# RMSNorm and projection with Strassen-like products: crossbar transposes in three pieces, and a new order for the head

## The chip, the cores and the metric

The kernel runs on one core of one Trainium2 chip. The metric is device time in microseconds (us) of one execution. A run consists of several executions, and the median of three is given for the kernel before.

## The reference

`x` has the shape (8, 1024, 768), that is 8192 rows of 768; `w_qkv` is 768 x 2304; all in float32. Each row is divided by its root mean square, scaled by `gamma`, and multiplied by the weights:

```python
rms = np.sqrt(np.mean(x ** 2, axis=-1, keepdims=True) + eps)
x_norm = x / rms * gamma
return np.matmul(x_norm, w_qkv).astype(np.float32)
```

The output is 8192 x 2304 in float32, 75.5 MB; the input is 25.2 MB, the weights 7.1 MB.

## The kernel before, in words

**Tiles.** The rows are cut into 64 tiles of 128. `load_x` (line 371) brings a tile in through SP's DMA queue. `load_w` (376) brings the weights in 16 pieces, and `conv` (382 to 386) multiplies them by `gamma` and makes them bf16, on VectorE, ScalarE or GpSimd as its last argument says.

**Tiles 0 to 3** go the plain way: cast, transpose on TensorE, `mm` against the bf16 weights (line 450, 512 or 256 columns), `evac` with the row's scale, `store`.

**Tiles 4 to 63** go in 30 pairs (2 to 31). A pair's 256 rows and 768 contraction elements form a 2 x 2 matrix of blocks; the weights, in three column chunks `c` of 768, form another. Seven products of blocks instead of eight give the result (Winograd's form of Strassen's algorithm). For the weights, `bound`, `fold`, `bound_tr`, `bound_top`, `bound_all` and `scales` find one scale per chunk, `quad` (548 to 552) makes four f16 quadrants, and `tsum` (558) four differences of quadrants. For the rows, `pstat` and `prms` on ScalarE and `precip` on VectorE give the row scales; `pcast` (582, VectorE) writes the scaled tile as f16 into `xb`; `pxbar` (586) transposes it by DMA from `xb` to `xT`, a crossbar transpose of 128 x 768; `osum` (600) makes the four sums s1 to s4 of `xT` blocks, on GpSimd in the steady state. s1 needs the whole odd tile, s4 comes last. `product` (620) is three matmuls of 128 x 384 into PSUM; products 1, 2 and 4 read `xT` itself, 5, 6, 3 and 7 read s1, s2, s4 and s3. `hold` (627, 629), `join` (638) and `last` (642) take results out of PSUM, and `pstore` (648) writes 384 KB, or half of it, to the output.

**What sets the order.** Every operation is entered with a time, and operations are emitted sorted by it. The time is only a sort key: each engine then runs its instructions in that order as their inputs come. For the first pairs the keys stand in a list, `PLAN`, which also delays some stores of early tiles to the end of the head. From pair 12 (`STEADY`) on a rule gives them: pair p and chunk c begin at z = `HEAD_END` + 7 slots for each chunk since pair 12, where a slot (three matmuls) is 0.4875 us, so that a pair has 21 slots or 10.24 us; everything else stands at z plus so many slots. All DMAs of tiles, weights, transposes and outputs are issued by SP, in one queue. Buffers: 9 of `x_t`, 4 of `xb`, 10 of `xT`, 3 of the sums, 12 of `ot`.

Of the kernel before, what the change touches and what calls it, by code (L numbers as in the profile page):

```python
# [15 lines left out]
HEAD_END = 134.61  # L16
# [3 lines left out]
    (0.000, "load_x", 1), (1.100, "load_x", 2), (1.460, "load_w", 4), (1.820, "load_x", 0), (2.180, "load_x", 3),  # L20
    (4.790, "cast", 1, "DVE"), (4.791, "gamma_in"), (4.792, "load_w", 2), (4.793, "stat", 1), (6.130, "recip", 1),
    (6.131, "load_w", 3), (6.132, "cast", 2, "ACT"), (6.440, "conv", 4, 5, "POOL"), (6.441, "idle", 3),
    (6.442, "load_w", 1), (6.820, "stat", 2), (6.821, "load_w", 0), (9.081, "conv", 2, 3, "POOL"), (9.082, "stat", 3),
    (9.083, "load_w", 6), (9.084, "idle", 6, 512), (9.085, "tr", 1), (9.086, "cp", 1, "DVE"),
    (9.761, "conv", 3, 4, "POOL"), (9.762, "stat", 0), (11.722, "conv", 0, 0, "ACT"), (11.723, "cast", 0, "DVE"),
    (11.724, "load_w", 7), (11.725, "cast", 3, "DVE"), (11.726, "conv", 1, 2, "POOL"), (11.727, "idle", 5, 512),
    (11.728, "mm", 1, 0, "5"), (11.729, "tr", 2), (11.730, "tr", 0), (11.731, "cp", 2, "DVE"), (11.732, "tr", 3),
    (11.733, "mm", 2, 0, "5"), (11.734, "mm", 1, 0, "3"), (11.735, "cp", 0, "DVE"), (11.736, "mm", 2, 0, "3"),
    (11.737, "mm", 0, 0, "5"), (11.738, "mm", 0, 0, "3"), (11.739, "mm", 0, 0, "4"), (11.740, "mm", 1, 0, "4"),
    (11.741, "recip", 0), (11.742, "cp", 3, "DVE"), (11.743, "mm", 2, 0, "4"), (11.744, "mm", 1, 0, "2"),  # L30
    (13.042, "conv", 6, 2, "POOL"), (13.043, "conv", 0, 1, "DVE"), (13.044, "mm", 0, 0, "2"),
    (13.045, "mm", 0, 0, "01"), (13.046, "bound", 0, 1, "DVE"), (13.047, "mm", 1, 0, "01"),
    (13.365, "mm", 2, 0, "012"), (13.832, "recip", 2), (13.833, "conv", 6, 3, "ACT"), (13.972, "bound", 0, 0, "ACT"),
    (14.013, "mm", 0, 512, "23"), (14.444, "mm", 1, 512, "23"), (14.445, "load_w", 5), (15.572, "evac", 1, 0, "ACT"),
    (15.573, "evac", 2, 0, "DVE"), (15.574, "mm", 2, 512, "23"), (15.575, "conv", 7, 5, "DVE"),
    (15.576, "conv", 7, 4, "POOL"), (15.577, "evac", 0, 0, "DVE"), (15.578, "mm", 3, 512, "23"),
    (15.739, "mm", 0, 512, "54"), (16.171, "mm", 3, 512, "45"), (16.172, "load_w", 9), (16.173, "conv", 5, 0, "DVE"),
    (16.603, "mm", 1, 512, "45"), (16.604, "conv", 5, 1, "POOL"), (16.605, "bound", 0, 2, "ACT"),
    (17.035, "mm", 3, 512, "01"), (17.036, "bound", 1, 0, "DVE"), (17.466, "mm", 2, 512, "45"),
    (17.467, "conv", 9, 3, "POOL"), (17.898, "mm", 1, 512, "01"), (17.899, "load_w", 8), (18.330, "mm", 2, 512, "01"),  # L40
    (18.761, "mm", 0, 512, "01"), (18.762, "fold", 0), (18.763, "conv", 8, 0, "ACT"), (19.193, "bound_tr", 0),
    (19.194, "conv", 9, 2, "POOL"), (19.195, "evac", 1, 512, "DVE"), (19.513, "bound_top", 0),
    (19.514, "mm", 3, 1024, "23"), (19.745, "mm", 0, 1024, "23"), (20.177, "bound_all", 0),
    (20.178, "conv", 8, 1, "POOL"), (20.179, "evac", 2, 512, "ACT"), (20.180, "bound", 1, 1, "ACT"),
    (20.297, "mm", 0, 1024, "01"), (20.298, "load_w", 10), (20.728, "mm", 2, 1024, "23"),
    (20.729, "conv", 10, 4, "POOL"), (20.730, "recip", 3), (20.731, "evac", 3, 512, "DVE"), (20.732, "load_x", 5),
    (20.733, "scales", 0), (20.953, "evac", 0, 512, "DVE"), (20.954, "load_w", 13), (21.160, "mm", 1, 1024, "23"),
    (21.613, "quad", 0, "b12", "DVE"), (21.614, "conv", 10, 5, "POOL"), (22.353, "conv", 13, 5, "DVE"),
    (22.354, "mm", 2, 1024, "01"), (22.355, "bound", 1, 2, "ACT"), (22.356, "mm", 0, 1024, "45"),
    (22.455, "mm", 2, 1024, "45"), (22.456, "load_w", 12), (22.783, "evac", 0, 1024, "DVE"),  # L50
    (22.784, "quad", 0, "b22", "POOL"), (23.443, "fold", 1), (23.444, "mm", 1, 1024, "01"),
    (23.445, "mm", 3, 1024, "45"), (23.446, "load_x", 4), (23.750, "mm", 3, 1024, "01"), (24.182, "bound_tr", 1),
    (24.183, "quad", 0, "b11", "DVE"), (24.184, "pstat", 5), (24.502, "bound_top", 1),
    (24.503, "conv", 13, 4, "POOL"), (24.504, "evac", 3, 1024, "ACT"), (24.722, "tsum", 0, "t1", "DVE"),
    (24.723, "load_w", 11), (24.724, "mm", 0, 1536, "45"), (24.733, "mm", 1, 1024, "45"),
    (25.587, "conv", 11, 0, "DVE"), (25.588, "pstat", 4), (25.952, "conv", 11, 1, "ACT"), (25.953, "load_x", 6),
    (25.954, "conv", 12, 2, "POOL"), (25.955, "bound_all", 1), (26.017, "tsum", 0, "t3", "DVE"),
    (26.018, "mm", 2, 1536, "45"), (26.592, "prms", 2), (26.593, "mm", 1, 1536, "45"),
    (26.594, "conv", 12, 3, "POOL"), (26.842, "evac", 1, 1024, "ACT"), (26.843, "mm", 3, 1536, "45"),
    (26.844, "mm", 1, 1536, "23"), (27.012, "mm", 3, 1536, "23"), (27.444, "mm", 0, 1536, "01"),  # L60
    (27.875, "mm", 0, 1536, "23"), (27.876, "evac", 2, 1024, "ACT"), (27.877, "load_w", 15), (27.878, "load_x", 7),
    (28.042, "pstat", 6), (28.043, "precip", 2), (28.044, "pcast", 4), (28.045, "scales", 1), (29.012, "pstat", 7),
    (29.013, "mm", 2, 1536, "23"), (29.014, "load_w", 14), (29.015, "pcast", 5), (29.016, "pxbar", 4),
    (29.017, "mm", 1, 1536, "01"), (29.018, "tsum", 0, "t2", "POOL"), (29.019, "pxbar", 5),
    (29.982, "evac", 1, 1536, "ACT"), (29.983, "conv", 15, 4, "DVE"), (29.984, "quad", 0, "b21", "POOL"),
    (29.985, "conv", 15, 5, "POOL"), (29.986, "mm", 3, 1536, "01"), (29.987, "conv", 15, 3, "POOL"),
    (29.988, "mm", 2, 1536, "01"), (30.034, "mm", 3, 0, "012345"), (30.035, "bound", 2, 1, "DVE"),
    (30.582, "prms", 3), (30.583, "evac", 0, 1536, "DVE"), (31.242, "precip", 3), (31.482, "pcast", 6),
    (32.032, "pcast", 7), (32.033, "mm", 3, 2048, "345"), (32.034, "load_x", 10), (32.035, "load_x", 11),
    (32.036, "mm", 2, 2048, "345"), (32.037, "conv", 14, 1, "POOL"), (32.172, "pxbar", 6),  # L70
    (32.173, "mm", 1, 2048, "345"), (32.174, "conv", 14, 0, "POOL"), (32.175, "conv", 14, 2, "POOL"),
    (32.582, "evac", 3, 0, "DVE"), (33.242, "osum", 2, "s1", "DVE"), (33.243, "mm", 2, 2048, "012"),
    (33.244, "store", 1, 1, 1024, 1024), (33.562, "osum", 2, "s3", "DVE"), (33.563, "mm", 0, 2048, "345"),
    (33.564, "product", 2, 0, 1), (33.882, "osum", 2, "s2", "DVE"), (33.883, "bound", 2, 0, "ACT"),
    (33.884, "pxbar", 7), (33.885, "load_x", 12), (33.886, "mm", 0, 2048, "012"), (33.887, "mm", 3, 2048, "012"),
    (33.888, "evac", 3, 1536, "ACT"), (34.202, "evac", 2, 2048, "DVE"), (34.203, "mm", 1, 2048, "012"),
    (34.204, "load_x", 13), (34.436, "product", 2, 0, 2), (34.602, "evac", 0, 2048, "DVE"),
    (34.924, "product", 2, 0, 5), (34.925, "quad", 1, "b12", "POOL"), (34.926, "hold", 2, 0, "a", "p1", "ACT"),
    (35.124, "join", 2, 0, 0, 0, "b", "p1"), (35.125, "bound", 2, 2, "ACT"), (35.411, "product", 2, 0, 6),
    (35.412, "load_x", 9), (35.413, "quad", 1, "b11", "POOL"), (35.899, "product", 2, 1, 1),  # L80
    (35.900, "evac", 1, 2048, "ACT"), (35.901, "fold", 2), (35.902, "quad", 1, "b22", "POOL"),
    (36.144, "hold", 2, 0, "c", "p5", "ACT"), (36.145, "osum", 2, "s4", "DVE"), (36.386, "product", 3, 1, 1),
    (36.874, "bound_tr", 2), (36.875, "evac", 3, 2048, "ACT"), (36.876, "tsum", 1, "t1", "DVE"),
    (36.877, "quad", 1, "b21", "POOL"), (37.194, "bound_top", 2), (37.195, "product", 3, 0, 1),
    (37.481, "product", 2, 0, 3), (37.482, "hold", 2, 0, "a", "u2", "ACT"), (37.483, "tsum", 1, "t2", "DVE"),
    (38.114, "osum", 3, "s3", "DVE"), (38.115, "hold", 2, 1, "a", "p1", "ACT"), (38.116, "product", 2, 1, 5),
# [216 lines left out]
def kernel(  # L303
# [8 lines left out]
    nc = tc.nc  # L312
# [14 lines left out]
    P = 128  # L327
# [412 lines left out]
```

## Time and profile before

| | us |
|---|---|
| median of 3 runs | 375.63 (372.15 to 376.89) |
| the profiled execution | 373.2 |
| its span in the profile | 371.1 |

| engine | busy us | share of the span |
|---|---|---|
| TensorE matmul (PE) | 345.1 | 93% |
| VectorE (DVE) | 275.0 | 74% |
| ScalarE (ACT) | 247.0 | 67% |
| GpSimd (POOL) | 145.5 | 39% |

The profile is one execution. Its page has the busy share of each engine in 40 slices of the span, the DMA queues, the chain of work that ended last (followed back from the last instruction, at each step to what released it) and the costliest groups of instructions by source line. The trace behind the page can be asked for instructions in order of time, for busy time in chosen stretches, and for waits. SPq is SP's queue: its rows are the issuing of DMAs, not their transfer. The times from issue to landing are in the page's last part:

```profile
out_dram<-ot SPq DMA_DIRECT2D x178, 384.0 KB, 4.9
x_t<-in_x_dram SPq DMA_DIRECT2D x64, 384.0 KB, 5.3
...
xT<-xb SPq DMA_TRANSPOSE x60, 5.4
```

The queue that carries them all is in the third part (packets, bytes, and the time that their packets took, as a share of 16 engines' span):

```profile
q1 hardware_dynamic: 89248, 119.56, 99.2%
```

### The profile page before, as it was taken

What the parts mean: (1) busy time and instruction counts of PE and PEld (TensorE: products, weight loads), DVE (VectorE), ACT (ScalarE), POOL (GpSimd) and SP (SyncE); (2) the same over time, 40 slices, a digit from 0 to 9 for tenths busy, and PEclk for the clock granted to TensorE, in tenths of its full rate; (3) what the DMA queues carried; (4) which work ended last, traced back from release to release, by engine and by line L of the source; (5) the groups of instructions that cost most, each with busy time, mean ns of one, the idle gap of its engine ahead of it and who ended that gap; (6) DMA issues with size and microseconds to landing.
All of it is one profiled execution on the core that took longest, in us unless ns stands there. A gap on an engine that the chain in (4) does not pass through costs nothing.

```text
span 371.1 us, 6579 instructions
## 1 busy us (share of the span) xinstructions
PE 345.1 (93%) x2055; PEld 199.6 (54%) x2055; DVE 275.0 (74%) x482; ACT 247.0 (67%) x495; POOL 145.5 (39%) x151
## 2 busy tenths in 40 slices
PE   5899796989799989999699999999999999999994
PEld 2445353555456546565366665666666666666662
DVE  2789999867467657777287777788787878777762
ACT  4697675657647757577367766776776677677543
POOL 1479795433132134430344423242444444345300
PEclk9999999999989999999899999999999999999999
DMA  7995986999989999999999999999999999997765
GB/s 256 391 388 133 310 323 189 300 267 388 256 320 356 294 392 394 307 378 347 395 309 377 350 304 356 335 388 331 354 362 336 347 344 377 316 380 259 253 256 213
DMA packets 89294, 119.98 MB, mean 323 GB/s; under 512 B 52390, under 2 KB 54188, under 8 KB 89260
## 3 DMA queue, kind: packets, MB, share of 16 engines
q1 hardware_dynamic: 89248, 119.56, 99.2%
q8 instruction: 16, 0.26, 0.3%
q14 instruction: 18, 0.15, 0.1%
q10 hardware_dynamic: 12, 0.00, 0.0%
HBM read 32.25 MB, written 75.50 MB: 290 GB/s over the span
## 4 chain that ended last, share of the span: by engine, by line
PE 67%; DMA 22%; DVE 6%; issue 2%; POOL 1%; SPq 1%; ACT 0%; DVEq 0%; POOLq 0%
PE pm L620 67%; DMA xT<-xb 8%; DMA out_dram<-ot 7%; DMA wq<-in_w_qkv_dram 5%; DVE xb L582 2%; DVE ot L638 2%; DMA x_t<-in_x_dram 2%; POOL su L600 1%; DVE su L600 1%; DVE bnd L507 0%; DVE wq L558 0%; DVE ot L466 0%; DVE w_b L382 0%; SPq L371 0%; DVE os L466 0%
## 5 line engine op out<-in xcount | busy, mean ns | idle before, releaser
L620 PE MATMUL pm<-wq,su 128*128 128x384 f16 x1080 | 208.3, 329 | 7.3 <-POOL su L600 5.1
L638 DVE SCALAR_TENSOR_TENSOR ot<-pm,sc,pp 128x384 f32<-128x384 f32 x270 | 155.4, 613 | 55.1 <-PE pm L620 40.3
L620 PE MATMUL pm<-wq,xT 128*128 128x384 f16 x810 | 162.5, 327 | 8.3 <-DVE ot L638 6.9
L629 ACT ACTIVATE pp<-pm,sc 128x384 f32<-128x384 f32 x214 | 121.0, 581 | 68.5 <-PE pm L620 61.8
L620 PEld LDWEIGHTS <-su 128*128 128x128 f16 x1080 | 105.3, 99 | 82.2 <-POOL su L600 8.0
L600 POOL TENSOR_TENSOR su<-xT 128x384 f16<-128x384 f16 x54 | 51.3, 970 | 183.4 <-DMA xT<-xb 131.7
L620 PEld LDWEIGHTS <-xT 128*128 128x128 f16 x810 | 79.2, 98 | 61.9 <-issue 10.3
L642 ACT ACTIVATE ot<-pm,sc 128x384 f32<-128x384 f32 x90 | 52.3, 581 | 41.2 <-PE pm L620 39.2
L582 DVE TENSOR_SCALAR xb<-x_t,rstd 128x768 f16<-128x768 f32 x60 | 52.4, 875 | 1.0
L627 DVE TENSOR_SCALAR pp<-pm,sc 128x384 f32<-128x384 f32 x56 | 34.3, 614 | 24.8 <-PE pm L620 24.6
L568 ACT ACTIVATE sq<-x_t 128x768 bf16<-128x768 f32 x60 | 50.0, 834 | 0.3 <-DMA x_t<-in_x_dram 0.3
L600 POOL TENSOR_TENSOR su<-xT,su 128x384 f16<-128x384 f16 x28 | 28.4, 1014 | 3.3 <-DVE su L600 1.2
L450 PE MATMUL pm<-w_b,xT 128*128 128x512 bf16 (+1 forms) x120 | 25.0, 358 | 1.1 <-ACT w_b L384 0.6
L600 POOL TENSOR_TENSOR su<-su,xT 128x384 f16<-128x384 f16 x27 | 25.0, 927 | 0.0
L386 POOL TENSOR_SCALAR w_b<-wq,g_sb 128x512 bf16<-128x512 f32 (+1 forms) x20 | 13.6, 692 | 13.3 <-DMA wq<-in_w_qkv_dram 13.3
L450 PEld LDWEIGHTS <-xT 128*128 128x128 bf16 x120 | 11.3, 98 | 12.7 <-issue 2.0
L558 POOL TENSOR_TENSOR wq<-wq 128x1152 f16<-128x1152 f16 x6 | 15.0, 2500 | 4.3 <-DVE wq L558 4.2
L552 POOL TENSOR_SCALAR wq<-w_b,inv 128x1152 f16<-128x1152 bf16 x9 | 12.8, 1430 | 2.5 <-DVE inv L536 2.5
L568 ACT ACTIVATION_READ_ACCUMULATOR sq<-x_t 128x1 f32 x60 | 11.5, 191 | 0.0
L510 ACT ACTIVATE sq<-w_b 128x1536 bf16<-128x1536 bf16 x6 | 8.9, 1475 | 1.2 <-DVE w_b L382 1.1
L572 ACT ACTIVATE rms<-ssq,eps_sb 128x2 f32<-128x2 f32 x30 | 8.8, 295 | 0.9
L466 DVE TENSOR_SCALAR ot<-pm,rstd 128x512 f32<-128x512 f32 x8 | 5.9, 742 | 0.4 <-PE pm L450 0.3
(47 smaller groups left out, 68.5 us busy)
## 6 DMA issues: line engine op xcount, KB each, us to landing
out_dram<-ot SPq DMA_DIRECT2D x178, 384.0 KB, 4.9
x_t<-in_x_dram SPq DMA_DIRECT2D x64, 384.0 KB, 5.3
wq<-in_w_qkv_dram SPq DMA_DIRECT2D x10, 512.0 KB, 9.3
out_dram<-ot SPq DMA_DIRECT2D x8, 512.0 KB, 5.7
wq<-in_w_qkv_dram SPq DMA_DIRECT2D x4, 256.0 KB, 7.4
xT<-xb SPq DMA_TRANSPOSE x60, 5.4
wq<-in_w_qkv_dram SPq DMA_DIRECT2D x2, 384.0 KB, 9.6
out_dram<-ot SPq DMA_DIRECT2D x4, 192.0 KB, 2.8
```

Source lines behind the costliest of these rows:

```text
L386: nc.gpsimd.tensor_scalar(out=o, in0=i, scalar1=g, scalar2=1.0, op0=mult, op1=mult)
L450: nc.tensor.matmul(out=PM[t, n0][:, :nl], lhsT=XT[t][:, ko, :], rhs=w_b[:, ko, n0:n0 + nl], start=(b == 1), stop=(b == KO))
L552: nc.gpsimd.tensor_scalar(out=o, in0=quad_view(c, q), scalar1=INV[c], scalar2=1.0, op0=mult, op1=mult)
L558: (nc.vector if eng == "DVE" else nc.gpsimd).tensor_tensor(out=new_quad(c, q), in0=i0, in1=i1, op=sub)
L568: nc.scalar.activation(out=sq, in_=X[t], func=AF.Square, accum_out=SS[p][:, t % 2:t % 2 + 1])
L582: nc.vector.tensor_scalar(out=XB[t], in0=X[t], scalar1=SS[t // 2][:, t % 2:t % 2 + 1], scalar2=None, op0=mult)
L600: (nc.vector if eng == "DVE" else nc.gpsimd).tensor_tensor(out=block(p, q), in0=block(p, x), in1=block(p, y), op=op)
L620: nc.tensor.matmul(out=PB[k][:, :CW], lhsT=block(p, a)[:, ko, :], rhs=WQ[c, b][:, ko, :], start=(first and ko == 0), stop=(ko == KO // 2 - ...
L627: nc.vector.tensor_scalar(out=o, in0=pb, scalar1=SC[c], scalar2=None, op0=mult)
L629: nc.scalar.activation(out=o, in_=pb, func=AF.Copy, scale=SC[c], bias=0.0)
L638: nc.vector.scalar_tensor_tensor(out=result(p, c, i, j), in0=PB[p, c, bank][:, :CW], scalar=SC[c], in1=PART[p, c, held], op0=mult, op1=add)
L642: nc.scalar.activation(out=result(p, c, 1, 0), in_=PB[p, c, "a"][:, :CW], func=AF.Copy, scale=SC[c], bias=0.0)
```

## The change

`pxbar` takes a second argument: it issues a third of a tile's transpose, two of its six 128 x 128 blocks, into the same `xT` buffer. The rule of the steady state spreads the three over other times, and puts the sums' key half a slot later. `PLAN` is replaced as a whole; `HEAD_END` follows from it.

```diff
-HEAD_END = 134.61
+HEAD_END = 135.96
...
-    (29.013, "mm", 2, 1536, "23"), (29.014, "load_w", 14), (29.015, "pcast", 5), (29.016, "pxbar", 4),
-    (29.017, "mm", 1, 1536, "01"), (29.018, "tsum", 0, "t2", "POOL"), (29.019, "pxbar", 5),
...
+    (30.634, "conv", 15, 5, "ACT"), (30.635, "pxbar", 5, 2), (30.636, "pxbar", 5, 0), (30.637, "mm", 3, 1536, "23"),
...
+    (30.641, "tsum", 0, "t2", "DVE"), (30.642, "mm", 3, 1536, "01"), (30.643, "pxbar", 4, 0),
...
-    def pxbar(t):
-        XT[t] = xTp.tile([P, KO, P], f16, name="xT")
-        nc.sync.dma_start_transpose(out=XT[t], in_=XB[t])
+    def pxbar(t, j):
+        if t not in XT:
+            XT[t] = xTp.tile([P, KO, P], f16, name="xT")
+        k0, k1 = 2 * j, 2 * j + 2
+        nc.sync.dma_start_transpose(out=XT[t][:, k0:k1, :], in_=XB[t][:, k0 * P:k1 * P])
...
-                    when(-28 + 7 * i + 2.3, pxbar, t)
+                    for j in range(3):
+                        when(((-25.7, -24.4, -22.6), (-18.7, -16.2, -13.0))[i][j], pxbar, t, j)
...
-                    when(-7 + 0.01 * i, osum, p, q, "POOL")
+                    when(-6.5 + 0.01 * i, osum, p, q, "POOL")
```

In the steady state the order on SP's queue over one pair's time was: transpose, load, store, store, transpose, store, store, load, store, store. It is now: piece, piece, load, piece, store, store, piece, piece, then the last piece just before or just after the next store, store, load, store, store.

The new `PLAN` also gives work to other engines. Over the whole kernel:

| operation | before | after |
|---|---|---|
| `conv` | GpSimd 20, VectorE 6, ScalarE 4 | GpSimd 14, VectorE 10, ScalarE 6 |
| `quad` | GpSimd 9, VectorE 3 | GpSimd 6, VectorE 4, ScalarE 2 |
| `tsum` | GpSimd 6, VectorE 6 | GpSimd 1, VectorE 11 |
| `osum` | GpSimd 109, VectorE 11 | GpSimd 113, VectorE 7 |
| `bound` | ScalarE 6, VectorE 3 | ScalarE 7, VectorE 2 |
| `evac` | ScalarE 10, VectorE 10 | ScalarE 11, VectorE 9 |
| `cp` | VectorE 4 | ScalarE 2, VectorE 2 |
| `cast` | VectorE 3, ScalarE 1 | VectorE 4 |
| `hold` | ScalarE 214, VectorE 56 | ScalarE 212, VectorE 58 |

The delayed stores of early tiles that stand after `HEAD_END` - 1 are, before, three of 128 KB and four of 384 KB; after, two of 512 KB, one of 128 KB and six of 384 KB.

## The prediction

> **What bounds the kernel.** I read the engine shares first, then the chain of waits, then a table by stage. The shares (PE 93%, DMA queue 99.2% of sixteen engines) name two candidates and settle nothing. The chain, in order of time, is cut here to its DMA waits and its last link (start, length, what):
>
> ```profile
> 86.23 4.03 DMA out_dram<-ot
> ...
> 124.42 6.96 DMA xT<-xb
> ...
> 145.39 7.55 DMA xT<-xb
> ...
> 155.19 8.01 DMA xT<-xb
> ...
> 163.22 7.51 DMA out_dram<-ot
> ...
> 171.29 6.93 DMA xT<-xb
> ...
> 179.34 185.68 PE pm L620 x1131
> ```
>
> From 179 us PE runs alone to the end; what goes before is broken by transposes that land late and stores that free their buffers late. The table by stage shows what that costs (busy us and instructions per engine, clock, DMA share, GB/s):
>
> ```profile
> 20.00:60.00 40.00, 34.37 (x190) 17.39 (x189) 38.78 (x64) 28.83 (x56) 32.61 (x26) 1.00 0.83 265
> ...
> 80.00:100.00 20.00, 17.66 (x107) 10.30 (x106) 12.48 (x22) 13.59 (x27) 7.33 (x8) 1.00 1.13 360
> 100.00:120.00 20.00, 18.33 (x104) 10.61 (x104) 13.74 (x26) 11.11 (x25) 5.70 (x7) 0.91 0.92 311
> 120.00:140.00 20.00, 18.23 (x111) 10.40 (x110) 13.24 (x25) 12.87 (x27) 5.19 (x6) 1.00 1.08 348
> ...
> 160.00:180.00 20.00, 16.35 (x101) 9.53 (x99) 12.81 (x23) 12.32 (x26) 5.39 (x6) 1.00 1.08 362
> 180.00:200.00 20.00, 20.00 (x114) 11.59 (x113) 13.49 (x25) 12.28 (x25) 7.48 (x9) 0.92 1.07 356
> 200.00:220.00 20.00, 20.00 (x125) 12.04 (x123) 15.54 (x28) 14.76 (x30) 6.09 (x7) 1.00 1.08 321
> ```
>
> Three regimes. Up to about 65 us VectorE is full (38.78 of 40 us) and the DMAs are not (0.83). From 70 to 190 the DMA queue is full, and PE falls short: 107+104+111+123+101+114 = 660 matmuls in 80 to 200 us, where six slices of 125 would be 750; 90 x 0.16 us = 14.4 us are lost there, some 3.4 of it to the clock of 0.91 and 0.92. From 200 us PE makes 125 matmuls in 20 us, one per 160 ns, and the DMAs just keep up. A pair of tiles then lasts 10.24 us. Nothing in the change shortens a matmul, so all gain must come from before 200 us, and a loss can come from anywhere.
>
> **The head, laid out anew.** VectorE is slow there because of GpSimd. VectorE's rows:
>
> ```profile
> 53.18 4.20 DVE L582 TENSOR_SCALAR xb<-x_t,rstd 128x768 f16<-128x768 f32 x2
> ...
> 60.79 2.23 DVE L582 TENSOR_SCALAR xb<-x_t,rstd 128x768 f16<-128x768 f32 x1
> ...
> 63.59 0.61 DVE L582 TENSOR_SCALAR xb<-x_t,rstd 128x768 f16<-128x768 f32 x1
> ```
>
> and GpSimd's at the same time:
>
> ```profile
> 54.44 2.54 POOL L558 TENSOR_TENSOR wq<-wq 128x1152 f16<-128x1152 f16 x1
> 60.23 2.37 POOL L558 TENSOR_TENSOR wq<-wq 128x1152 f16<-128x1152 f16 x1 [3.26 <-DVE wq L558]
> ```
>
> The same cast takes 2.23 us beside a GpSimd subtraction and 0.61 us without. Setting each VectorE form in 20 to 60 us against its fast instances (20th percentile) gives 8.8 us of such excess, beside 32.6 us of GpSimd work. Before the first product of pair 5 the new order takes from GpSimd 6 conversions (0.69 us each), 3 weight quadrants (1.43) and 5 weight differences (2.50): 20.9 us; it adds four sums (0.95): 3.8. That leaves 15.5 of 32.6 us, and the excess in proportion: 8.8 x 15.5/32.6 = 4.2, a gain of 4.6 us. VectorE takes on 5 differences (0.70), 4 conversions (0.56), a quadrant and a cast and sheds sums, a bound, two copies and some joins: by those durations 50.2 us becomes 52.4, a loss of 2.2. Net -2.4 us on the engine that carries the chain there. ScalarE takes on some 6 us (49.6 to 55.6) and has 11 us idle in these 40. Bounds: -6 (the added work falls into waits) to +3 (no excess goes, ScalarE becomes late).
>
> **Each transpose as three.** In the steady state SP's queue looks so (start, length):
>
> ```profile
> 253.81 2.22 SPq L586 DMA_TRANSPOSE xT<-xb  x1
> 256.12 1.02 SPq L648 DMA_DIRECT2D out_dram<-ot  x2
> 257.19 0.46 SPq L371 DMA_DIRECT2D x_t<-in_x_dram  x1
> ```
>
> SP's issue time. A transpose issues in 1.21 us at least and 1.47 in the median, a plain DMA in 0.37 to 0.43. A piece lies between 0.40 (a third) and 1.21 (all of it fixed). I take 0.65: 0.37 that any DMA costs and a third of the other 0.84, since plain loads of 384 and 512 KB differ by 0.03 only and the extra must be the transposing. Per pair SP then needs 6 x 0.65 + 8 x 0.41 = 7.2 us instead of 2 x 1.47 + 3.3 = 6.2, of 10.24. The idle 4 us cover it: cost 0.
>
> Transfer time. The trace's DMA records show a transpose as 768 packets of 256 bytes, 18 ns each: 0.86 us over 16 engines; a piece is 256 packets, 0.29 us, so the sum stays. But the 60 transposes last 80.2 us from first to last packet, not 51.6: in 28.6 us fifteen engines wait for one that is late. What makes it late is mostly instruction fetch (37 packets of 8 and 16 KB, 26.4 us, each on one engine). Of the loss some 12 us lie in 70 to 190 us. In a whole transpose the early engines do some 28 of 48 packets before they stop; a piece gives each only 16, so an early engine may finish it and go on to a store. Bounds: -12 (all absorbed) to +12 (the late engine is met twice). I take -3: a quarter, since two pieces in a row (32 packets) stop it again.
>
> The Trainium skill ("DMA: Bandwidth & Descriptors", Rules for kernel authors) speaks against the change: coalesce, since under 64 KB one pays mostly overhead; its bandwidth table has 64 KB at 0.95 us. A piece is just 64 KB; at 0.95 us, 180 pieces would be an estimated 171 us of queue, some 90 more than the 80 now, and the full queue would carry the kernel to some 460 us. No row here shows such a size alone; in a full queue the neighbours hide the start, so the sum goes by the packets.
>
> More waits. In the built program each DMA on SP's queue waits for the one eight issues earlier. Ten DMAs per pair make that 8.2 us of lead, fourteen make it 5.85, against landings of 4.9 to 5.4 in the median and up to 8.0. Where the queue is full SP will stop more often, with stores and loads queued behind; but seven others are still in flight (at the least six pieces and a store, 2.7 us, against 1.2 from issue to first packet), so the DMAs do not run dry. Cost 0, bound +2.
>
> **Stores and order behind it.** Of the early tiles' delayed stores 3.5 MB instead of 2.0 stand after the head: 1.5 MB, four transfers of 0.97 us, move from the full queue before it to the full queue after it. Cost 0, since both stretches are bound by the same queue; bound +4, if they push pair 14's transposes further back, where the chain already waits 6.93 us for one.
>
> The last piece is later. Of an odd tile it moves from -18.7 to -13.0 slots of 0.4875 us, 2.8 us, behind or just before a store (0.97 us in the queue). In pairs 15 to 29 GpSimd's fourth sum ends 0.41 to 2.39 us after the pair's first product, and product 3 needs it at 2.44: slack 0.05 to 2.0. With 0.97 more, the tightest pairs stall up to 0.9 us. A stall lets the queue drain, so I count it once: +1, bound +19 (20 pairs at 0.97). Starting the sums at -6.5 slots instead of -7 changes no order on GpSimd: 0. Extra instructions: 120 issues with their waits, about one fetch more, +0.5.
>
> **Sum.** -2.4 - 3 + 1 + 0.5 = -4 us. The profiled execution took 373.2 us (span 371.1 and 2.1 around it), so 369.2; its kernel's median is 375.63, 2.4 higher, which puts the same change at 371.6. I predict 371.
>
> **Rivals.** (1) Absorbed: pieces free the early engines throughout, and VectorE loses its excess: its added work in waits: -12 - 4.6 + 1.5 = -15.1, 360. For it: most transposes that meet no late engine last 0.75 to 0.86 us. Against: a clustered piece meets the same barrier. (2) Slower by SP: the issue time does not shrink. It decides from (10.24 - 3.3)/6 = 1.16 us a piece; at 1.21 a pair takes 10.54, +0.3 x 27 pairs = +8, 384; at the present loaded mean of 1.65, +79. For it: loaded issues of 2.2 to 2.9 us. Against: the large gap to a plain DMA. (3) Slower by the sums: the DMAs have no spare capacity and each steady pair pays for its late last piece, 0.4 to 0.97 us x 20 = +8 to +19, 384 to 395. For it: the queue is never empty between 110 and 330 us. Against: transposes there wait 2.4 to 4.5 us without growing. (4) Nothing: from 70 to 190 us the DMAs set the pace, and a shorter head only makes PE wait longer there: 374 to 377.
>
> **Chances.** 2% (7.5 us) is about what a measurement here tells from no change, which puts the borders at 368.1 and 383.1. Forecast 0.46 (363 to 376; 0.18 of it below 368.1), absorbed 0.17, SP 0.13, late sums 0.16 (0.14 over the border), nothing 0.08. Faster 0.18 + 0.17 = 0.35; slower 0.13 + 0.14 = 0.27; within 0.38. The range 360 to 386 leaves out half of rival 1, the dear half of 2 and 3.
>
> **What will show it.** Transposes x180 with an issue mean of about 0.65 us, and SP idle per pair of some 3 us; VectorE's casts in 20 to 60 us near 0.6; more than 660 matmuls in the 120 us after the head; 125 per 20 us at the end. Wrong if a piece issues in over 1.1 us, if the steady state shows fewer than 125 matmuls with GpSimd's sums as releaser, or if the head ends later than before.

## The result, and the profile after

| | before | after |
|---|---|---|
| median, us | 373.89 of 4 runs (371.15 to 376.89) | 471.31 of 4 runs (469.70 to 472.79) |
| span of the profiled execution, us | 371.1 | 469.9 |

By the medians the change costs 97 us. The ratio is 1.27, with a 95% interval of 1.2628 to 1.2772. (Ratios here and below are not quotients of the medians, since they leave out executions that ran long at a lower clock, and two of the experiments below, `e12_sp_transposes` and `e12b_act`, have only a profile of such an execution, so that of their pages only who waits for whom is used.) The forecast was 371, in a range of 360 to 386.

The page of the changed kernel, from the third part the queue, from the fourth the chain of waits by engine, from the fifth the products that read sums and GpSimd's first two sums (busy us, mean ns, then idle us before them and what ended it), from the sixth the transposes (median us from issue to landing):

```profile
q1 hardware_dynamic: 93088, 119.58, 79.7%
...
PE 42%; DMA 23%; SPq 11%; POOL 9%; DVE 6%; issue 6%; ACT 1%; POOLq 0%; DVEq 0%
...
L630 PE MATMUL pm<-wq,su 128*128 128x384 f16 x1080 | 223.7, 343 | 64.1 <-POOL su L610 55.8
...
L610 POOL TENSOR_TENSOR su<-xT 128x384 f16<-128x384 f16 x57 | 51.3, 920 | 305.7 <-DMA xT<-xb 276.2
...
xT<-xb SPq DMA_TRANSPOSE x180, 3.1
```

The same two rows of the kernel before:

```profile
L620 PE MATMUL pm<-wq,su 128*128 128x384 f16 x1080 | 208.3, 329 | 7.3 <-POOL su L600 5.1
...
L600 POOL TENSOR_TENSOR su<-xT 128x384 f16<-128x384 f16 x54 | 51.3, 970 | 183.4 <-DMA xT<-xb 131.7
```

TensorE now waits 64.1 us for sums (7.3 before), and GpSimd waits 276.2 us for transposes (131.7 before, when that held up nobody for long). Yet the transfers have become easier, not harder: the queue is 79.7% busy where it was 99.2%; a piece lands 3.1 us after its issue, a whole transpose landed after 5.4; and a store of the same 384 KB lands after 3.1 us, not 4.9. The data come late because they are asked for late. SP itself now stands in the chain with 11% (1% before).

The table by stage, same columns as before (PE, PE loads, VectorE, ScalarE, GpSimd, clock, DMA share, GB/s):

```profile
20.00:60.00 40.00, 34.33 (x184) 17.64 (x183) 32.53 (x63) 31.02 (x60) 19.14 (x18) 0.96 0.83 261
...
80.00:100.00 20.00, 18.99 (x103) 10.65 (x102) 12.70 (x23) 12.36 (x26) 3.58 (x4) 0.90 0.76 243
300.00:320.00 20.00, 15.06 (x81) 8.12 (x82) 9.49 (x18) 8.61 (x18) 7.12 (x8) 0.91 0.85 271
400.00:420.00 20.00, 14.47 (x84) 7.83 (x85) 10.35 (x19) 9.62 (x21) 7.12 (x8) 1.00 0.82 263
```

In 20 to 60 us VectorE is less busy (32.53 us, was 38.78), but TensorE made no more matmuls for it (184, was 190). From 80 to 460 us the slices of 20 us have 71 to 106 matmuls, with no recovery; the kernel before had 125 from 200 us on. The clock is not the cause, though it was lower (0.945 in the mean of the span, 0.991 before): the slice from 400 us has 84 matmuls at the full clock.

What SP does, first all its transposes, before and after (min, median, max ns), then its queue over one pair:

```profile
L586 SPq DMA_TRANSPOSE xT<-xb x60: 1212/1472/2955, 32.1 to 345.8; - x60
```

```profile
L596 SPq DMA_TRANSPOSE xT<-xb x180: 1167/1243/3757, 26.7 to 450.8; - x180
```

```profile
374.09 3.35 SPq L596 DMA_TRANSPOSE xT<-xb  x2
377.48 0.58 SPq L379 DMA_DIRECT2D x_t<-in_x_dram  x1
378.11 1.68 SPq L596 DMA_TRANSPOSE xT<-xb  x1
379.89 1.00 SPq L658 DMA_DIRECT2D out_dram<-ot  x2
380.99 2.67 SPq L596 DMA_TRANSPOSE xT<-xb  x2
383.75 0.62 SPq L658 DMA_DIRECT2D out_dram<-ot  x1
384.43 1.18 SPq L596 DMA_TRANSPOSE xT<-xb  x1
385.70 0.53 SPq L658 DMA_DIRECT2D out_dram<-ot  x1
386.29 0.42 SPq L379 DMA_DIRECT2D x_t<-in_x_dram  x1
386.80 0.91 SPq L658 DMA_DIRECT2D out_dram<-ot  x2
387.88 2.00 SPq L596 DMA_TRANSPOSE xT<-xb  x1
```

A piece issues in 1.243 us in the median; a whole transpose took 1.472. Each line begins within 0.2 us of the end of the one before: SP issues without a stop, and the pair, from 374.09 to the next pair's first piece at 387.88, lasts 13.8 us instead of 10.24.

### The profile page after: what moved, and what is told of

Read it like the earlier page. It is cut to its first block, busy times and chain, and to the rows that moved or that the text cites. A ratio compares the mean times of both kernels' runs of the same rounds, so it can differ in the third digit from the quotient of the medians.

```text
span 469.9 us, 6772 instructions
## 1 busy us (share of the span) xinstructions
PE 372.0 (79%) x2045; PEld 202.6 (43%) x2047; DVE 264.5 (56%) x487; ACT 251.4 (53%) x501; POOL 123.7 (26%) x141
## 3 DMA queue, kind: packets, MB, share of 16 engines
q1 hardware_dynamic: 93088, 119.58, 79.7%
## 4 chain that ended last, share of the span: by engine, by line
PE 42%; DMA 23%; SPq 11%; POOL 9%; DVE 6%; issue 6%; ACT 1%; POOLq 0%; DVEq 0%
PE pm L630 42%; DMA xT<-xb 11%; DMA out_dram<-ot 9%; POOL su L610 8%; SPq L596 8%; DVE ot L648 4%; DMA wq<-in_w_qkv_dram 3%; SPq L658 2%; DMA x_t<-in_x_dram 1%; DVE wq L566 1%; DVE xb L590 1%; SPq L379 1%; POOL w_b L394 1%; ACT pp L639 0%; ACT sq L576 0%
## 5 line engine op out<-in xcount | busy, mean ns | idle before, releaser
L630 PE MATMUL pm<-wq,su 128*128 128x384 f16 x1080 | 223.7, 343 | 64.1 <-POOL su L610 55.8
L630 PE MATMUL pm<-wq,xT 128*128 128x384 f16 x810 | 168.2, 337 | 23.4 <-DVE ot L648 21.4
L630 PEld LDWEIGHTS <-su 128*128 128x128 f16 x1080 | 106.8, 102 | 155.8 <-POOL su L610 74.3
L610 POOL TENSOR_TENSOR su<-xT 128x384 f16<-128x384 f16 x57 | 51.3, 920 | 305.7 <-DMA xT<-xb 276.2
L630 PEld LDWEIGHTS <-xT 128*128 128x128 f16 x810 | 81.1, 100 | 83.2 <-issue 31.5
L652 ACT ACTIVATE ot<-pm,sc 128x384 f32<-128x384 f32 x90 | 51.8, 581 | 65.6 <-PE pm L630 60.1
L590 DVE TENSOR_SCALAR xb<-x_t,rstd 128x768 f16<-128x768 f32 x60 | 41.6, 697 | 0.9
L610 POOL TENSOR_TENSOR su<-xT,su 128x384 f16<-128x384 f16 x28 | 26.0, 928 | 2.6 <-DVE su L610 0.5
L394 POOL TENSOR_SCALAR w_b<-wq,g_sb 128x512 bf16<-128x512 f32 (+1 forms) x14 | 10.2, 738 | 21.8 <-DMA wq<-in_w_qkv_dram 21.8
L566 DVE TENSOR_TENSOR wq<-wq 128x1152 f16<-128x1152 f16 x11 | 8.9, 812 | 0.0
L560 POOL TENSOR_SCALAR wq<-w_b,inv 128x1152 f16<-128x1152 bf16 x6 | 8.2, 1387 | 2.4 <-ACT pp L639 2.4
L390 DVE TENSOR_SCALAR w_b<-wq,g_sb 128x512 bf16<-128x512 f32 x10 | 4.6, 484 | 2.7 <-DMA wq<-in_w_qkv_dram 2.7
```

Of the source, the lines that this page charges most:

```text
L394: nc.gpsimd.tensor_scalar(out=o, in0=i, scalar1=g, scalar2=1.0, op0=mult, op1=mult)
L566: (nc.vector if eng == "DVE" else nc.gpsimd).tensor_tensor(out=new_quad(c, q), in0=i0, in1=i1, op=sub)
L590: nc.vector.tensor_scalar(out=XB[t], in0=X[t], scalar1=SS[t // 2][:, t % 2:t % 2 + 1], scalar2=None, op0=mult)
L610: (nc.vector if eng == "DVE" else nc.gpsimd).tensor_tensor(out=block(p, q), in0=block(p, x), in1=block(p, y), op=op)
L630: nc.tensor.matmul(out=PB[k][:, :CW], lhsT=block(p, a)[:, ko, :], rhs=WQ[c, b][:, ko, :], start=(first and ko == 0), stop=(ko == KO // 2 - ...
L652: nc.scalar.activation(out=result(p, c, 1, 0), in_=PB[p, c, "a"][:, :CW], func=AF.Copy, scale=SC[c], bias=0.0)
```

## The experiments

Three theories stand behind the expectations. I: SP's issue time, the same for a small transpose as for a large one, sets the pair. V: the number of transfers does, through the DMA engines or their queue. L: the sums wait for a last piece that comes late. The first four expectations also name II (the new order of the head is at fault), III (an early form of L) and IV (each DMA waits for the one eight issues earlier).

All readings of SP's queue are brought together here first. A pair's length is the mean distance between the first transposes of pairs that follow each other in the steady state; "in issues" adds up SP's DMA instructions, per pair; "idle" adds up, of every pause between two of SP's instructions, the part above 0.2 us. The rest of the pair is short gaps, 1.1 to 1.6 us. Taken over another stretch of the steady state, the figures move by 0.1 to 0.3 us.

| kernel | transposes a pair | median us | us a pair | in issues | idle |
|---|---|---|---|---|---|
| before | 2 | 373.9 | 10.25 | 6.74 | 1.92 |
| `e1_plan_whole` | 2 | 370.4 | 10.27 | 6.64 | 2.15 |
| `e7b_pair_new` | 1 | 363.2 | 10.32 | 6.01 | 2.94 |
| `e3_halves` | 4 | 413.0 | 12.20 | 11.04 | 0.02 |
| `e4_five_one` | 4 | 419.6 | 12.32 | 11.19 | 0.02 |
| after | 6 | 471.3 | 14.00 | 12.77 | 0.02 |
| `e2_old_three` | 6 | 482.0 | 14.31 | 13.13 | 0.02 |
| `e9_unused` | 6 | 470.1 | 14.12 | 12.87 | 0.02 |
| `e11_early` | 6 | 467.9 | 14.10 | 12.89 | 0.02 |
| `e15_pause_long` | 2, and 4 pauses | 467.6 | 13.73 | 6.72 + 5.53 | 0.13 |
| `e16_pause_short` | 2, and 4 pauses | 391.2 | 11.05 | 7.15 + 2.26 | 0.24 |

### Which part of the change

**`e1_plan_whole`**: the new order, without the split.

```diff
     def pxbar(t, j):
-        if t not in XT:
-            XT[t] = xTp.tile([P, KO, P], f16, name="xT")
-        k0, k1 = 2 * j, 2 * j + 2
-        nc.sync.dma_start_transpose(out=XT[t][:, k0:k1, :], in_=XB[t][:, k0 * P:k1 * P])
+        if t in XT:
+            return
+        XT[t] = xTp.tile([P, KO, P], f16, name="xT")
+        nc.sync.dma_start_transpose(out=XT[t], in_=XB[t])
```

> The changed kernel (its order of the head, its 14 slots of keys) with each tile's transpose whole again, at the key of the first piece. Theory I (a transpose costs SP about 1.2 us to issue whatever its size, so six per pair fill SP's queue): the loss goes, 366 to 380 us, and SP is busy under 70% of the steady state. Theory II (the new order of the head is at fault): it stays above 400 us. Theory III (the last piece comes too late behind a store): the loss goes too, as in I. Theory IV (every DMA waits for the one eight before it, and there were fourteen per pair): the loss goes, as in I.

**`e2_old_three`**: the order before, with the split, three pieces in a row.

```diff
-        nc.sync.dma_start_transpose(out=XT[t], in_=XB[t])
+        for k0 in (0, 2, 4):
+            nc.sync.dma_start_transpose(out=XT[t][:, k0:k0 + 2, :], in_=XB[t][:, k0 * P:(k0 + 2) * P])
```

> The kernel before, each transpose issued as three pieces one right behind the other, nothing between them, nothing else moved. Theory I: 180 issues at 1.2 to 1.5 us again, a pair takes 13 to 14 us in the steady state, 445 to 475 us. Theory III (late last piece): the last piece stands where the whole transpose stood, so 374 to 390 us. Theory II (new head): 374 to 390 us. Theory IV: fourteen DMAs per pair, the same as after, 440 to 475 us, but then SP's time would go into waits between issues, not into the issues.

**`e3_halves`**: the new order, two pieces of three blocks, at the first and second of a tile's three places (`n` counts them).

```diff
-        k0, k1 = 2 * j, 2 * j + 2
-        nc.sync.dma_start_transpose(out=XT[t][:, k0:k1, :], in_=XB[t][:, k0 * P:k1 * P])
+        if n < 2:
+            k0, k1 = 3 * n, 3 * n + 3
+            nc.sync.dma_start_transpose(out=XT[t][:, k0:k1, :], in_=XB[t][:, k0 * P:k1 * P])
```

> The changed kernel with two pieces of three blocks instead of three of two, at the keys of the first two pieces. Theory I: 120 issues of at least 1.17 us; SP per pair 4 x 1.5 plus 3.6 for stores and loads plus gaps = 10 to 10.6 us against PE's 10.24, so just at the edge: 372 to 395 us, not halfway (420). If the cost grows with the blocks in a piece, an issue takes under 0.9 us. Theory V (the sum of the transposes' lost time grows with the number of pieces): halfway between, about 420 us.

**`e4_five_one`**: the order before, one piece of five blocks and one of one block.

```diff
-        nc.sync.dma_start_transpose(out=XT[t], in_=XB[t])
+        nc.sync.dma_start_transpose(out=XT[t][:, :5, :], in_=XB[t][:, :5 * P])
+        nc.sync.dma_start_transpose(out=XT[t][:, 5:, :], in_=XB[t][:, 5 * P:])
```

> The kernel before, each transpose as a piece of five blocks and one of one block right behind it, on two lines of the source, so that each size has its own row. Theory I: both rows have a minimum of 1.17 to 1.25 us although one moves five times the data; 120 issues, 374 to 395 us. If the cost grows with the blocks: about 1.1 us and 0.5 us, and the time stays within 372 to 380.

Against 373.44 us of the kernel before on the same chip: `e1_plan_whole` 370.38 (ratio 0.9887, 0.9795 to 0.9979), `e2_old_three` 481.99 (1.292, 1.2822 to 1.3019), `e3_halves` 412.98 (1.1044, 1.0961 to 1.1128), `e4_five_one` 419.55 (1.1225, 1.1145 to 1.1305).

The new order costs nothing; it seems to gain about 1%, but the interval reaches from 0.2 to 2%. The split alone costs everything, whether other transfers stand between the pieces or not; the changed kernel, which has them between and the new order too, is 11 us cheaper. `e3_halves` and `e4_five_one` were expected at 372 to 395 and 374 to 395 by theory I and missed: two transposes more in a pair already cost 40 to 46 us. `e3_halves` came nearer to theory V's "about 420", so these two runs do not speak against V. The issue times themselves came as theory I has them. In `e4_five_one`, five blocks and one block (min, median, max ns):

```profile
L586 SPq DMA_TRANSPOSE xT<-xb x60: 1223/2102/2717, 30.9 to 396.2; - x60
```

```profile
L587 SPq DMA_TRANSPOSE xT<-xb x60: 1212/1220/1948, 32.3 to 397.7; - x60
```

1.223 us at the least for five blocks, 1.212 for one: the size hardly enters. The medians differ by place: the five blocks come behind several plain DMAs, the one block behind the five. The miss lay in what I had added up beside them. The table shows it: SP idles 1.92 us a pair before the change, not 4, since gaps take 1.6 us. And when SP runs without pause the issues grow, the first transpose of a tile to some 2.1 us, plain DMAs from 0.43 us in the mean to 0.57. So four transposes a pair fill SP as six do.

### The number of issues, or what waits for them

**`e9_unused`**: the new order, whole transposes, and where the second and third piece stood a transpose of one block that nobody reads.

```diff
         if t in XT:
+            spare = xtra.tile([P, 1, P], f16, name="xs")
+            nc.sync.dma_start_transpose(out=spare, in_=XB[t][:, :P])
             return
```

> The changed order with whole transposes (370.4 us), and at the places of the second and third piece a transpose of one 128x128 block into a tile that nobody reads: 180 issues as in the changed kernel, a third more bytes of transposes, and not one product that waits for the added ones. Theory I (SP's issue time, the same for a small transpose as for a large one): SP is as full as in the changed kernel, so 455 to 480. Theory L (the loss is that the sums wait for a last piece that comes late): 370 to 385, since the data comes whole with the first transpose.

**`e11_early`**: the changed kernel with the squares, casts and pieces of a pair (not its loads) seven slots earlier in the steady state; the cut lines move the squares and the row scales.

```diff
-                        when(((-25.7, -24.4, -22.6), (-18.7, -16.2, -13.0))[i][j], pxbar, t, j)
+                        when(((-32.7, -31.4, -29.6), (-25.7, -23.2, -20.0))[i][j], pxbar, t, j)
...
-                    when(-28 + 7 * i + 0.9, pcast, t)
+                    when(-35 + 7 * i + 0.9, pcast, t)
...
```

> The changed kernel with the squares, casts and pieces of pair 12 on seven slots (3.4 us) earlier in the order; every issue stays on SP. Theory I: SP runs through its 13.8 us a pair without pause, and the order within it does not shorten it: 466 to 474. Theory L (late pieces): 430 to 450, as the pieces lead their sums by 3.4 us more.

`e9_unused` took 470.13 us (1.2578, 1.2493 to 1.2663), the changed kernel's own time, though every product has its data with the first, whole transpose. The added ones:

```profile
L596 SPq DMA_TRANSPOSE xs<-xb x120: 1093/1185/2513, 30.4 to 451.9; - x120
```

`e11_early` took 467.94 us (1.2515, 1.2433 to 1.2597): a lead of 3.4 us more gives back 3 us of 97. For the changed kernel theory L falls. The loss goes with the number of transposes issued; that suits theory I and theory V alike, so it takes the runs below to part these two.

### Fewer issues

**`e6_pair`** (the order before) and **`e7b_pair_new`** (the new order): one transpose for both tiles of a pair, whose `xb` and `xT` lie side by side. The lines are cut from `e6_pair`; `e7b_pair_new` keeps one transpose a tile up to pair 4.

```diff
+        if t % 2 == 0:
+            return
+        for i in (t - 1, t):
+            XT[i] = half(xTp, XT2, i, [P, 2 * KO, P], f16, "xT")
+        nc.sync.dma_start_transpose(out=XT2[t // 2], in_=XB2[t // 2])
```

> The kernel before, with one transpose for the two tiles of a pair (128x1536, 30 issues in place of 60), issued where the second tile's was; the tiles of xb and xT lie in pairs for it. Theory I: the issue still takes some 1.2 us at the least, so SP's 68% of the steady state falls to some 57%; SP was not the bound, so the time stays at 370 to 376; the first tile's rows come about 7 slots (3.4 us) later than they did, but the second's, which the sums wait for, no later. Theory V (engine time by the number of transfers): 30 fewer transfers give back part of the 28.6 us by which the transposes' packets stand apart, so 355 to 368. Against both: a transfer of 12 blocks lands later than one of 6 (5.4 us in the trace of before, perhaps 8 to 10), and the sums that wait for it start later: 380 to 400.

> The changed order with one transpose for the two tiles of a pair from pair 5 on, issued where the second tile's first piece was (pair 4 and before keep one a tile). The pair in the order before gave 370.4 us, the whole transposes in the changed order 370.4 against 373.4 before. Theory I: SP is not the bound in either, so 366 to 372; a longer transfer that makes the sums late would give 375 to 390.

`e6_pair` took 370.44 us (0.994, 0.9901 to 0.998), as theory I had it and not in theory V's 355 to 368: SP was not the bound. `e7b_pair_new` took 363.24 us (0.9689, 0.9618 to 0.9759), faster than both kernels and 3 us better than theory I's range. (Theory V, on record before `e6_pair` was measured, had 350 to 364 for this order with pairs, and 363 lies in that. By the DMA records the transposes' packets take 83.2 us over sixteen engines here and 88.4 in `e1_plan_whole`, so a part of the 7 us between the two may be due to the transfers.) Its page, the chain by engine:

```profile
PE 68%; DMA 18%; SPq 4%; DVE 4%; POOL 2%; ACT 2%; issue 2%; DVEq 0%; ACTq 0%; POOLq 0%
```

It reaches 125 matmuls in 20 us already at 80 us, once (the kernel before 107 there). The order by itself gave 1.1% (0.2 to 2.1), the pairing by itself 0.6% (0.2 to 1.0), both together 3.1% (2.4 to 3.8). Whether that is more than the sum, and why, no run parts.

### Issues taken off SP

If SP's issue time is the cause, taking other issues off SP should give the time back. Seven kernels tried it; all keep the 180 pieces except `e14_whole_pool`. The moves hold from tile 14 and pair 5 on.

**`e5_loads_act`**: the changed kernel, loads of `x` from ScalarE's queue. **`e8_five_act`**: also the stores of the odd tile.

```diff
-        nc.sync.dma_start(out=X[t], in_=xf[t * P:(t + 1) * P, :])
+        (nc.scalar if t >= 14 else nc.sync).dma_start(out=X[t], in_=xf[t * P:(t + 1) * P, :])
...
-        nc.sync.dma_start(out=of[t * P:(t + 1) * P, n0 + CW * j0:n0 + CW * j1], in_=OUT[t, "s", c][:, CW * j0:CW * j1])
+        (nc.scalar if i == 1 and p >= 5 else nc.sync).dma_start(out=of[t * P:(t + 1) * P, n0 + CW * j0:n0 + CW * j1], in_=OUT[t, "s", c][:, CW * j0:CW * j1])
```

> The changed kernel, with the loads of x of tile 14 onward issued from ScalarE's queue instead of SP's; nothing else moves, the same transfers of the same sizes. Theory I (SP's issue time): two issues of 0.61 us leave SP's 13.8 us per pair, so a pair takes about 12.6 us; over the 27 pairs that were late that is 1.2 x 27 = 33 us, so about 438 us (430 to 446). Theory V (the transfers themselves keep the DMA engines, by their number): the number and the size of the transfers are as before, so 465 to 475. A cost to both: a load that waits on ScalarE's queue would hold its evictions; ScalarE is busy 53%, so none is expected.

> As the kernel with the loads of x on ScalarE's queue, and the three stores of a pair's second tile go there too, each behind ScalarE's own last operation of that tile; SP keeps six transposes and three stores a pair. Theory I: SP's 13.8 us a pair lose 1.22 + 3 x 0.46 = 2.6 us, so 11.2 us a pair, and 2.6 x 27 = 70 us of the loss come back: about 400 us (385 to 410). Theory V: 465 to 475, since not one transfer is gone. ScalarE's own work, some 6 us of a pair, and five issues of some 0.5 us stay under 10.24.

**`e10_five_early`**: `e8_five_act` with the seven slots of `e11_early`.

> The kernel with the loads of x and three of six stores of a pair on ScalarE's queue (431.6 us), and from pair 12 on the squares, casts and pieces of a pair seven slots (3.4 us) earlier in the order. That kernel had SP at 87%, with waits for casts and joins between the issues, and 12.0 us a pair. Theory L (relieved of its issues, SP is held by a round: a store waits for its join, the pieces behind it come late, the sums and products after them, then the next join): the lead breaks the round, a pair takes 10.5 to 11 us, and 20 pairs x 1.0 to 1.5 = 20 to 30 us come back: 400 to 412. Theory I alone (SP's issue time sets the pair): 426 to 434.

**`e12_sp_transposes`**: `e10_five_early` with the even tile's stores from GpSimd's queue. **`e12b_act`**: all stores and loads on ScalarE's. SP has the transposes alone; these two and the next two keep the seven slots.

```diff
-        (nc.scalar if i == 1 and p >= 5 else nc.sync).dma_start(out=of[t * P:(t + 1) * P, n0 + CW * j0:n0 + CW * j1], in_=OUT[t, "s", c][:, CW * j0:CW * j1])
+        (nc.sync if p < 5 else nc.scalar if i == 1 else nc.gpsimd).dma_start(out=of[t * P:(t + 1) * P, n0 + CW * j0:n0 + CW * j1], in_=OUT[t, "s", c][:, CW * j0:CW * j1])
```

> The kernel with loads and half the stores on ScalarE's queue and the pieces seven slots earlier (415.7 us; SP 91% busy, a pair in 11.4 us), with the other three stores of a pair from GpSimd's queue: from tile 14 and pair 5 on SP issues the six transposes of a pair and nothing else. The transfers are as many and as large as in the changed kernel. Theory I (SP's issue time): six issues of 1.24 to 1.38 us are 7.4 to 8.3 us of 10.24, SP is no longer the bound, the pair goes back to 10.2 to 10.5 us, and the time to 375 to 392. Theory V (the small transfers keep the DMA engines or their queue): 405 to 420. A cost to both that the trace has not shown: an issue by GpSimd may hold the sums behind it.

> As the last, with all six stores and both loads of a pair on ScalarE's queue. SP again has the six transposes alone. ScalarE's own work of a pair is some 6.2 us, and eight issues of some 0.5 us make 10.2 of 10.24, with stores that wait for VectorE's joins ahead of evictions. Theory I: 380 to 405, by ScalarE. Theory V: 410 to 425.

**`e13_plain_pool`**: all stores and loads on GpSimd's queue. **`e14_whole_pool`**: the same with whole transposes.

> The changed kernel with pieces seven slots earlier, and from tile 14 and pair 5 on every load of x and every store from GpSimd's queue: SP issues the six transposes of a pair alone, and no engine that evicts or casts issues a transfer. Six issues of 1.25 us are 7.5 us of SP's 10.24; GpSimd has eight issues of 0.55 us (from the kernel with three of them there) and sums of 3.7 us, 8.1 us, and holds the sums behind stores that wait. Theory I (the issue's time on SP): 375 to 395, and within 10 us of the same kernel with whole transposes. Theory V (the small transfers themselves): 405 to 425, and over 30 us more than with whole transposes. In the two runs before this SP stood still for casts (30.6 us and 55.2 us of 130), and ScalarE for the landing of transposes at its own loads and stores (34.3 and 56.1 us in all): by theory I that wait is what kept those two slow.

> The last kernel with whole transposes in place of the pieces, every other queue and time the same: what GpSimd's queue costs without the split. 366 to 385 by both theories, unless GpSimd, with some 8.1 us a pair and stores that wait for joins, makes the sums late: then both runs are slow, and the difference of the two decides: under 10 us by theory I, over 30 us by theory V.

| kernel | median us | ratio, 95% interval | us a pair | SP idle a pair |
|---|---|---|---|---|
| `e5_loads_act` | 454.14 | 1.2165 (1.206 to 1.2269) | 13.32 | 0.22 |
| `e8_five_act` | 431.63 | 1.1628 (1.1544 to 1.1713) | 11.70 | 0.51 |
| `e10_five_early` | 415.69 | 1.1117 (1.1038 to 1.1197) | 11.15 | 0.13 |
| `e12_sp_transposes` | 425.69 | 1.1299 (1.1176 to 1.1422) | | |
| `e12b_act` | 458.55 (450.27 to 459.24) | none | | |
| `e13_plain_pool` | 466.53 | 1.2464 (1.2304 to 1.2624) | 13.35 | 2.31 |
| `e14_whole_pool` | 434.15 | 1.1264 (1.116 to 1.1368) | 11.38 | 4.30 |

(The lengths and pauses of the last two depend on the stretch taken, by up to 1 us.) The first three go theory I's way, since not one transfer is gone and up to 56 us come back. Two of them bring back less than theory I expected. `e10_five_early`, the test of theory L, lies between I alone (426 to 434) and L (400 to 412): the lead, which gave 3 us while SP was full, gives 16 here, so once SP is partly relieved late pieces do count. The next two are plain misses of theory I: with nothing but transposes on SP the time rises again, and `e12_sp_transposes` came nearer to theory V's 405 to 420. The profile shows a new wait there. In `e10_five_early` the waits of ScalarE show it (us, times, longest):

```profile
ACT pp L639 <- DMA xT<-xb: 20.8, 6, 6.4
```

ScalarE does not read a pair's `xT`. But in the built program loads and stores on ScalarE's queue draw on the same eight completion semaphores as SP's transposes (the trace has the same eight numbers for both), and each waits until the DMA eight before it has landed. So it seems that ScalarE stops at its store, and its eviction (`pp`) behind it comes late. The changed kernel has no such line. In `e12_sp_transposes` and `e12b_act` it is there again, and SP stands waiting for casts. That this wait is what kept them slow is argued; no run takes it away alone. GpSimd's queue is no way out: even with whole transposes, plain DMAs there cost 13%. On that footing the pieces cost some 45 us more by the ratios (32 by the medians), and over 30 was to speak for theory V: by the measure set beforehand this pair of runs went V's way. I don't count it, for reasons found afterwards: the runs of either kernel lie 17 to 30 us apart, in both GpSimd stood at stores that waited for VectorE (11 and 18 us of 130), and SP's six issues took 10.1 us a pair, not the 7.5 expected, so SP was not free. The first three speak for theory I against V; the other four decide nothing.

### The same time without the transfers

**`e15_pause_long`** and **`e16_pause_short`**: `e1_plan_whole`, and where the second and third piece stood 24 or 10 increments of a semaphore that nobody waits for.

```diff
         if t in XT:
+            for _ in range(24):
+                nc.sync.sem_inc(spare, 1)
             return
```

> The changed order with whole transposes (370.4 us), and at the places of the second and third piece 24 increments of a semaphore that nobody waits for, on SP: at the 53 ns that stand between two such instructions in the trace, 1.27 us, as long as SP takes for a piece (1.243 us in the median), with no transfer behind it. Theory I (SP's time, whatever fills it): a pair's issues in that kernel take some 6.9 us and their gaps 0.9; 4 x 1.27 = 5.1 more make 12.9 us, 2.7 over 10.24, times 27 pairs 72 us: about 442 us, up to 465 if the other issues grow as SP runs without pause. Theory V (the small transfers behind the issues): no transfer is added, so 368 to 380.

> The last kernel with 10 increments in place of 24: 0.53 us a place, 2.1 us a pair, so SP has 7.8 + 2.1 = 9.9 us of 10.24 to do. Theory I: just under the point from which it decides, 370 to 385. Theory V: 368 to 378. It is there to show that the loss of the last begins where SP is full and not with the first instruction added.

`e15_pause_long` took 467.60 us (1.2529, 1.2451 to 1.2607), a little over theory I's dear end and nearly 90 us over theory V's. An increment took 59 ns, not 53, so a pause is 1.38 us. SP's queue there (the increments are not listed; a pause is the gap behind a line):

```profile
343.54 2.18 SPq L599 DMA_TRANSPOSE xT<-xb  x1
347.21 0.34 SPq L379 DMA_DIRECT2D x_t<-in_x_dram  x1
349.06 0.82 SPq L661 DMA_DIRECT2D out_dram<-ot  x2
349.98 1.58 SPq L599 DMA_TRANSPOSE xT<-xb  x1
```

The transpose ends at 345.72 and SP comes to the load at 347.21; the next pause lies between 347.55 and 349.06. With 60 transposes, as before the change, and SP held by other means, the loss is the same: SP's time alone is enough to explain it, and a part for the transfers is not needed. `e16_pause_short` took 391.19 us (1.047, 1.0376 to 1.0565) where 370 to 385 was expected. I had counted 9.9 us of 10.24 on SP; by the table the spare time was 2.15 us and the pauses take 4 x 0.56 = 2.26, and the transposes beside them grew from 1.71 to 1.94 us in the mean. So SP was just overfull, and the loss is small: by these two runs it begins about where SP's spare time ends.

## Why the prediction was wrong

**The step that failed** is the issue time of a piece: "I take 0.65: 0.37 that any DMA costs and a third of the other 0.84". It measured 1.243 us in the median and 1.49 in the mean of the steady state, so SP, put at 7.2 us of 10.24 and at no cost, needs 12.77 us of issues a pair and became the bound. The argument was that the part above a plain DMA must be the transposing, hence go with the size. It hardly does: the least issue is 1.09 us for one block (1.21 in another kernel), 1.17 for two, 1.18 for three, 1.22 for five, 1.21 for six. Of the two bounds given, 0.40 and 1.21, the upper one, which had the whole issue fixed, was nearly right for the median and too low for the mean. The choice between them failed, since the row it went by (plain loads of two sizes) belongs to another instruction. The prediction's own signs of being wrong came: a piece issued in over 1.1 us, and the steady state fell under 125 matmuls with GpSimd's sums as releaser.

**"The idle 4 us cover it."** They were 1.9. The sum put the issues at 6.2 us where they take 6.74, and left out 1.6 us of gaps between them. With 10.25 us a pair, 1.6 of gaps and 3.4 of plain DMAs, six pieces fit only under (10.25 - 1.6 - 3.4) / 6 = 0.88 us each, not 1.16. At 0.65 it would still have gone well by that sum, so the first step decides.

**Rival 2** ("the issue time does not shrink") happened, and had a chance of 0.13. Its dear end, the loaded mean of 1.65 us and +79 us, was nearer than its cheap end of 384. The measured mean is lower, 1.49; what makes up for it is the gaps, which the rival left out, and plain DMAs of 0.50 us instead of 0.41. In the sum of the table, 27 pairs x (14.00 - 10.25) = 101 us; measured, 97.

**The head**: -2.4 us. Right in kind, by the new order alone (`e1_plan_whole`, against the row of 20 to 60 us in the prediction):

```profile
20.00:60.00 40.00, 38.05 (x219) 20.76 (x217) 36.49 (x71) 34.81 (x70) 21.15 (x19) 1.00 1.04 309
```

GpSimd fell from 32.61 to 21.15 us, VectorE from 38.78 to 36.49, a cast there from 1.44 to 0.61 us in the median, and TensorE made 219 matmuls, not 190. The kernel is 3.1 us under the one before. That this is so near to -2.4 may be luck: the interval is wide, and the run also holds the moved stores and the later sums.

**Transfers**: -3, with -12 and +12 as bounds. The mechanism did work; what it is worth in time is not decided. Both kernels move 46,080 packets of 256 bytes for their transposes. By the DMA records these took 80.9 us over sixteen engines before and 54.0 after, where 18 ns each would make 51.8, so nearly all of the 28.6 us that the prediction found lost is gone. An emptier queue is not the reason: with whole transposes and a queue 83.5% busy (`e15_pause_long`) they take 79.7. And `e2_old_three`, with the pieces in a row, takes 64.9: pieces in a row do stop engines again, as the prediction feared. But all packets of the queue together take 375 us of sixteen engines, 368 before, since those of loads and stores grew (the 3,072-byte ones from 249.9 to 279.0). So the DMA engines have no more to do that would explain 97 us, and no gain in time either could be seen: no run has pieces and a free SP (`e13_plain_pool` comes near, and there GpSimd was late).

**By the Trainium skill** ("DMA: Bandwidth & Descriptors", Rules for kernel authors) the estimate had been some 460 us, close to 471. That is luck: it was a full queue of transfers at 0.95 us (the table's figure for loads from HBM that GpSimd issues), and the trace has a queue that is not full. A rule that meets the case stands on another page, which I had not weighed: "Perfetto Trace Analysis", What "DMA-bound" means, counts the issuing sequencer as a bound of its own, to be known by a track that is solid with DMA slices. SP's track after the change agrees, with 12.77 of 14.00 us in DMA issues and 0.02 idle. The first page's remark that issue time is usually small beside the transfer (Issuing engines are not separate DMA queues) does not hold here: 1.24 us of issue against 0.29 us that a piece's packets take of sixteen engines (it lands 3.1 us after the issue).

**Waits of eight, 0**: held on SP. It has no pauses for them (idle 0.02 us), and the issues hold none either: wherever the trace of the changed kernel gives the landing of the DMA eight before, in 246 issues from 150 to 430 us, it lies at least 2.1 us before the issue's start. The waits struck where DMAs went to a second queue. **The last piece, +1**: not tested. `e11_early` gains 3 us by leading it by 3.4, but SP was full all the while. **Stores and fetches**: too small to be seen beside the rest.

## What to carry to other kernels

Count DMA instructions on a queue before bytes: here a crossbar transpose of one to six blocks costs its issuing engine 1.1 to 1.2 us at the least, so fewer and larger ones are the way, down to one for a pair of tiles. Read an engine's spare time from the gaps of its own timeline, not as the span less the shortest durations. And to part an instruction's time from what it sets off, put the same time there without the effect: the pauses showed in two runs what seven rearrangements had left open, that SP's time is enough to make the loss.

## What the runs showed of the hardware

- A transpose of twelve blocks (`e6_pair`) issues in 1.38 us at the least; in the steady state, always behind eight plain DMAs, in 1.9 at the least and 2.56 in the mean. Six blocks took 1.21 at the least, so above six the size begins to enter.
- In the changed kernel the first piece of a tile, behind two or more plain DMAs, issues in 2.0 us (even tile) or 1.8 (odd tile) in the median, a piece behind another piece in 1.24, a piece behind a single plain DMA mostly in 1.17 to 1.19. With all plain DMAs on GpSimd's queue (`e13_plain_pool`) the mean is 1.7. Why is open.
- The 256-byte packets of a whole transpose cost 1.5 times as much DMA engine time as those of three pieces with other transfers between them (80.9 against 54.0 us over sixteen engines, for the same 46,080 packets).
- A store issues in 0.33 us at the least on SP and ScalarE, in 0.54 us on GpSimd; moved there, with the seven slots, loads and stores made even the kernel with whole transposes 13% slower than before (`e14_whole_pool`).
